# Attention: value products gathered into stretches of two to four token tiles

## The chip, the core and the metric

The kernel runs on one core of a Trainium2 chip. The metric is the device time of one execution in microseconds; a profile comes from one further execution, recorded with its instructions. Names of engines: PE is TensorE (PEld its weight loads), ACT is ScalarE, DVE is VectorE, POOL is GpSimd, SP is SyncE.

## The reference, cut to what matters

Two layers on 1024 tokens of width 1024, each with a mixer and a SwiGLU feed-forward block. The change lies in the first layer's mixer, two kinds of attention side by side, with 8 heads of 64 columns each:

```python
# heads A: softmax over the own chunk of 64 tokens and the 8 before it, learned relative bias
p = jax.nn.softmax(scores, axis=-1)
o = jnp.einsum('bhcqk,bckhd->bhcqd', p, vb)
# heads B: stick-breaking, strictly causal
log_beta = jax.nn.log_sigmoid(z)
log_1m_beta = jnp.where(causal, jax.nn.log_sigmoid(-z), 0.0)
after = lax.cumsum(log_1m_beta, axis=3, reverse=True) - log_1m_beta
w = jnp.where(causal, jnp.exp(log_beta + after), 0.0)
o = jnp.einsum('bhqk,bkhd->bqhd', w, v)
```

The outputs of all heads are joined and go through one output projection. The second layer's mixer is recurrent and, like the feed-forward blocks, isn't touched.

## The kernel before, in words

Heads are handled in pairs, in the order 4, 5, 6, 7, 0, 1, 2, 3 (`seq`): pairs 4 to 7 are the stick-breaking ones (called sigmoid pairs below, after their sigmoid), pairs 0 to 3 the softmax ones. For each pair `project(p)` makes queries and keys (L166 to L168, each product as three fp32r passes of 512 columns), and every second pair `v_tile` makes the values of two pairs (L291 to L293). Then `attend(p)` goes over 8 token tiles of 128 queries:

- scores for the two heads (L364, L365), as wide as the keys that the tile may see: `nb` blocks of 128 keys, 1 to 8 in a sigmoid pair, 1 to 5 in a softmax pair;
- the weights: in a sigmoid pair ScalarE's sigmoid (L372), GpSimd's causal mask (L381), VectorE's reverse scan (L384) and difference (L387); in a softmax pair VectorE's bias and minimum (L368), ScalarE's exponential (L376), VectorE's reciprocal, GpSimd's scaling (L379);
- the `2 * nb` blocks of 128 x 128 weights, two heads in turn, in groups of up to four: four transposes on TensorE into one PSUM tile `tr` of two (L397), a copy to the SBUF tile `pt` of three (L401 on ScalarE, L403 on VectorE for every second group of a softmax tile), and four value products (L406). A value product holds 64 columns of `v` in the array, those of head 0 in one half of it and those of head 1 in the other, and adds 64 rows of `pso`, one PSUM bank for four token tiles;
- after each fourth tile `pso` is copied to `ob` (L412) and stored.

A sigmoid pair has 20 groups, a softmax pair 18.

The order on each engine comes from a planner: the program is traced in the order of its text, and a simulated run of the machine then decides what each engine issues next. Among the instructions whose inputs are there by its clock, the one that stands first in the program goes first; so the projections of the next pair, which stand behind `attend(p)` in the program, are put wherever nothing of the pair itself is ready. TensorE then executes in that order. `issue_after(x)` adds an edge that keeps an instruction behind `x` on the same engine in the issue order; it is no wait for `x` to finish. `behind` does the same for a list. The last pair, 3, has no projections behind it; the output projection's first products (L497) follow.

Of the kernel before, what the change touches and what calls it, by code (L numbers as in the profile page):

```python
# [8 lines left out]
F32 = mybir.dt.float32  # L9
# [6 lines left out]
P = 128  # L16
# [83 lines left out]
class Trunk:  # L100
# [164 lines left out]
    def attention(self, x_src, w_in, bias_t, o_dst, hT):  # L265
        nc, tc = self.nc, self.tc
        with ExitStack() as ctx:
            ap = ctx.enter_context(tc.tile_pool(name="att", bufs=1, reuse_waits="tile"))
# [29 lines left out]
            def v_alloc():  # L298
                return [ap.tile([P, NT, P], F32, tag="v", bufs=3, name=self.uid("v")) for _ in range(2)]
# [27 lines left out]
            def attend(p, st, vt):  # L327
                bias = [None, None]
                if p < 4:
                    for h in range(2):  # L330
                        b = ap.tile([P, 640], F32, tag="bias", bufs=2, name=self.uid("bias"))
                        nc.sync.dma_start(b, bias_t[2 * p + h])
                        nc.gpsimd.tensor_scalar(b, b, -1.0, 1.0, op0=ALU.mult, op1=ALU.mult)
                        nc.gpsimd.memset(b[0:64, 576:640], BIG)
                        nc.gpsimd.memset(b[64:P, 0:64], BIG)
                        bias[h] = b
                for i in range(NT):
                    k0 = max(0, i - 4) if p < 4 else 0
                    nb = i + 1 - k0
                    n = nb * P  # L340
                    if i % 4 == 0:
                        ops = pp.tile([P, 512], F32, tag="o", bufs=1, name=self.uid("pso"))
                    nat = []
                    n_c = 1 if n <= 512 else 2
                    w = n // n_c
                    for h in range(2):
                        qs, k1, k2 = st[h]
                        q = qs[:, i * P:(i + 1) * P]
                        if p < 4 and h == 1:
                            pr = ap.tile([P, 640], F32, tag="nata", bufs=3, name=self.uid("pr"))  # L350
                        else:
                            pr = ap.tile([P, 1024], F32, tag="nat", bufs=4, name=self.uid("pr"))
                        if p < 4:
                            mn = [ap.tile([P, 1], F32, tag="mn", bufs=8, name=self.uid("mn")) for _ in range(n_c)]
                            sm = ap.tile([P, 1], F32, tag="sm", bufs=4, name=self.uid("sm"))
                        for c in range(n_c):
                            if p == seq[-1] and h == 1:

                                sc = prp.tile([P, 512], F32, tag="proj", bufs=2, name=self.uid("sc"))[:, :w]
                            else:  # L360
                                sc = pp.tile([P, 512], F32, tag="sc", bufs=3, name=self.uid("sc"))[:, :w]
                            ks = slice(k0 * P + c * w, k0 * P + c * w + w)
                            cs = slice(c * w, c * w + w)
                            nc.tensor.matmul(sc, q, k1[:, ks], start=True, stop=False)  # L364
                            nc.tensor.matmul(sc, q, k2[:, ks], start=False, stop=True)  # L365
                            if p < 4:
                                off = 640 - n + c * w
                                nc.vector.tensor_tensor_reduce(  # L368
                                    pr[:, cs], sc, bias[h][:, off:off + w], 1.0, 3e38,
                                    op0=ALU.add, op1=ALU.min, accum_out=mn[c])  # L370
                            else:
                                nc.scalar.activation(pr[:, cs], sc, AF.Sigmoid)  # L372
                        if p < 4:
                            if n_c == 2:
                                nc.vector.tensor_tensor(mn[0], mn[0], mn[1], op=ALU.min)
                            nc.scalar.activation(pr[:, :n], pr[:, :n], AF.Exp, bias=mn[0], scale=-1.0,  # L376
                                                 accum_out=sm)
                            nc.vector.reciprocal(sm, sm)
                            nc.gpsimd.tensor_scalar(pr[:, :n], pr[:, :n], sm, 1.0, op0=ALU.mult, op1=ALU.mult)  # L379
                        else:  # L380
                            nc.gpsimd.affine_select(pr[:, n - P:n], pr[:, n - P:n], pattern=[[-1, P]],  # L381
                                                    compare_op=ALU.is_gt, fill=1.0, base=0,
                                                    channel_multiplier=1)
                            nc.vector.tensor_tensor_scan(  # L384
                                pr[:, 0:n][:, ::-1], pr[:, 0:n][:, ::-1], self.zero.to_broadcast([P, n]),
                                1.0, op0=ALU.mult, op1=ALU.add)
                            nc.vector.tensor_tensor(pr[:, 0:n - 1], pr[:, 1:n], pr[:, 0:n - 1],  # L387
                                                    op=ALU.subtract)
                            nc.gpsimd.memset(pr[:, n - 1:n], 0.0)
                        nat.append(pr)  # L390
                    blocks = [(kb, h) for kb in range(nb) for h in range(2)]
                    for b0 in range(0, len(blocks), 4):
                        bl = blocks[b0:b0 + 4]
                        tr = pp.tile([P, 512], F32, tag="tr", bufs=2, name=self.uid("tr"))
                        pt = ap.tile([P, 512], F32, tag="pt", bufs=3, name=self.uid("pt"))
                        for j, (kb, h) in enumerate(bl):
                            nc.tensor.transpose(tr[:, j * P:(j + 1) * P], nat[h][:, kb * P:(kb + 1) * P],  # L397
                                                self.ident)
                        w = len(bl) * P
                        if p >= 4 or (b0 // 4) % 2 == 0:  # L400
                            nc.scalar.copy(pt[:, :w], tr[:, :w])  # L401
                        else:
                            nc.vector.tensor_copy(pt[:, :w], tr[:, :w])  # L403
                        for j, (kb, h) in enumerate(bl):
                            kt = k0 + kb
                            nc.tensor.matmul(  # L406
                                ops[h * 64:(h + 1) * 64, (i % 4) * P:(i % 4) * P + P],
                                vt[p % 2][:, kt, h * 64:h * 64 + 64],
                                pt[:, j * P:(j + 1) * P], start=kb == 0, stop=kb == nb - 1)
                    if i % 4 == 3:  # L410
                        ob = ap.tile([P, 512], F32, tag="ob", bufs=1, name=self.uid("ob"))
                        nc.scalar.copy(ob, ops)  # L412
                        nc.sync.dma_start(o_dst[p][:, (i // 4) * 512:(i // 4) * 512 + 512], ob)

            seq = [4, 5, 6, 7, 0, 1, 2, 3]
            vt = v_alloc()
# [25 lines left out]
            for t, x in enumerate(xt):  # L442
                h = ap.tile([P, D], F32, tag="st", bufs=12, name=self.uid("h0"))
# [18 lines left out]
            for j, p in enumerate(seq):  # L462
                attend(p, st, vt)
                if j < 7:
                    q = seq[j + 1]
                    if q % 2 == 0:
                        wv = v_weights(q // 2)
                        vt = v_alloc()
                        for t2 in range(4):
                            v_tile(q // 2, wv, vt, t2)  # L470
                    st = project(q)
# [675 lines left out]
```

## Time and profile before

| | us |
|---|---|
| median of 3 runs | 2225.85 |
| lowest, highest | 2224.5, 2227.01 |
| the profiled execution | 2226.18 |
| its span, first to last instruction | 2224.4 |
| mean granted TensorE clock | 0.996 |
| first and last value product start | 81.03, 513.9 |

The page gives busy time per engine over the span. A group of the groups' view is one line of the kernel on one engine with one shape: how many, its busy time, the mean length of one in ns, and the idle time of the engine ahead of it with what ended it. TensorE's lengths overlap, since matmuls are pipelined: the distance between two starts says what one holds the engine for. In TensorE's timeline instructions of one line that follow each other without a gap are put together (x8), so a row there is a run.

### The profile page before, as it was taken

What the parts mean: (1) busy time and instruction counts of PE and PEld (TensorE: products, weight loads), DVE (VectorE), ACT (ScalarE), POOL (GpSimd) and SP (SyncE); (2) the same over time, 40 slices, a digit from 0 to 9 for tenths busy, and PEclk for the clock granted to TensorE, in tenths of its full rate; (3) what the DMA queues carried; (4) which work ended last, traced back from release to release, by engine and by line L of the source; (5) the groups of instructions that cost most, each with busy time, mean ns of one, the idle gap of its engine ahead of it and who ended that gap; (6) DMA issues with size and microseconds to landing.
All of it is one profiled execution on the core that took longest, in us unless ns stands there. A gap on an engine that the chain in (4) does not pass through costs nothing. (4 is left out here: it accounts for less than half of the span.)

```text
span 2224.4 us, 30685 instructions
## 1 busy us (share of the span) xinstructions
PE 2191.2 (99%) x11198; PEld 1807.4 (81%) x11198; DVE 1537.5 (69%) x2496; ACT 1146.0 (52%) x2108; POOL 226.8 (10%) x458
## 2 busy tenths in 40 slices
PE   8999999999999999999999999999999999999998
PEld 8887888877788888888888687888788888888886
DVE  5776765464877777775866687636877777768675
ACT  4544455464865444442446568527755444434543
POOL 2111112131100000000001323201100000000011
PEclk9999999999999999999999999999999999999999
DMA  5101011124523333334648611246333333328566
GB/s 167 50 22 42 25 44 41 60 94 139 201 95 95 113 116 96 112 102 170 213 136 256 181 48 48 86 166 206 121 118 114 95 119 95 118 90 284 166 179 161
DMA packets 184393, 266.04 MB, mean 120 GB/s; under 512 B 13617, under 2 KB 114993, under 8 KB 184242
## 3 DMA queue, kind: packets, MB, share of 16 engines
q1 hardware_dynamic: 183602, 261.98, 37.5%
q8 instruction: 88, 1.44, 0.3%
q10 hardware_dynamic: 640, 2.10, 0.3%
q14 instruction: 63, 0.52, 0.1%
HBM read 198.49 MB, written 65.54 MB: 119 GB/s over the span
## 5 line engine op out<-in xcount | busy, mean ns | idle before, releaser
L646 PE MATMUL ps<-hS,q 128*128 128x512 f32 (+1 forms) x1288 | 489.7, 381 | 0.7 <-ACT hS L96 0.3
L647 PE MATMUL ps<-hS,q 128*128 128x512 f32 (+1 forms) x1288 | 489.0, 380 | 0.9 <-DVE hS L89 0.9
L648 PE MATMUL ps<-hS,q 128*128 128x512 f32 (+1 forms) x1288 | 488.4, 380 | 0.0
L617 DVE TENSOR_TENSOR q<-raw,q 128x512 fp32r<-128x512 f32 x308 | 204.5, 685 | 184.7 <-ACT q L616 184.2
L646 PEld LDWEIGHTS ps<-hS,q 128*128 128x128 f32 x1288 | 241.7, 188 | 47.9 <-ACT hS L96 0.7
L647 PEld LDWEIGHTS ps<-hS,q 128*128 128x128 f32 x1288 | 242.2, 188 | 47.3 <-DVE hS L89 1.3
L648 PEld LDWEIGHTS ps<-hS,q 128*128 128x128 f32 x1288 | 242.1, 188 | 45.8
L616 ACT CAST q<-raw 128x512 fp32r<-128x512 f32 x308 | 177.4, 615 | 157.6 <-DVE raw L625 133.2
L732 PE MATMUL ps<-o,o 128*128 128x512 f32 x616 | 239.9, 390 | 0.4 <-DVE o L727 0.2
L733 PE MATMUL ps<-o,o 128*128 128x512 f32 x616 | 238.0, 390 | 0.5 <-DVE o L861 0.5
L604 ACT ACTIVATE raw<-raw,gcol 128x256 f32<-128x256 f32 x352 | 150.3, 498 | 148.9 <-DMA raw<-in_ffn_w_up_dram 73.9
L731 PE MATMUL ps<-o,o 128*128 128x512 f32 x616 | 221.2, 391 | 3.6 <-ACT o L860 3.5
L726 ACT CAST o<-raw 128x512 fp32r<-128x512 f32 x184 | 110.6, 620 | 161.1 <-PE ps L733 51.1
L182 POOL TENSOR_SCALAR rs<-ss 128x1 f32<-128x1 f32 x60 | 32.9, 549 | 1447.1 <-ACT junk L178 1363.0
L727 DVE TENSOR_TENSOR o<-raw,o 128x512 fp32r<-128x512 f32 x184 | 123.1, 686 | 55.6 <-ACT o L726 54.9
L156 DVE TENSOR_TENSOR wlo<-raw,whi 128x1024 fp32r<-128x1024 f32 x76 | 93.0, 1225 | 71.4 <-ACT whi L155 70.1
L731 PEld LDWEIGHTS ps<-o,o 128*128 128x128 f32 x616 | 115.6, 188 | 29.3 <-ACT o L860 5.2
L733 PEld LDWEIGHTS ps<-o,o 128*128 128x128 f32 x616 | 115.7, 188 | 25.3 <-DVE o L861 1.4
L732 PEld LDWEIGHTS ps<-o,o 128*128 128x128 f32 x616 | 115.7, 188 | 25.0 <-DVE o L727 1.2
L155 ACT CAST whi<-raw 128x1024 fp32r<-128x1024 f32 x76 | 79.8, 1051 | 57.2 <-PE ps L167 20.2
L401 ACT COPY pt<-tr 128x512 f32<-128x512 f32 (+1 forms) x128 | 65.5, 528 | 80.3 <-PE tr L397 79.7
L166 PE MATMUL psq<-hT,whi 128*128 128x512 f32 x256 | 101.2, 395 | 1.1 <-DVE v L296 1.1
(202 smaller groups left out, 4336.9 us busy)
## 6 DMA issues: line engine op xcount, KB each, us to landing
raw<-in_ffn_w_gate_dram SPq DMA_DIRECT2D x44, 512.0 KB, 4.2
raw<-in_ffn_w_up_dram SPq DMA_DIRECT2D x44, 512.0 KB, 4.2
gS<-c SPq DMA_DIRECT2D x88, 256.0 KB, 3.9
raw<-gS SPq DMA_DIRECT2D x88, 256.0 KB, 2.8
gA<-c SPq DMA_DIRECT2D x66, 256.0 KB, 3.3
raw<-in_ffn_w_down_dram SPq DMA_DIRECT2D x63, 256.0 KB, 4.0
raw<-in_attn_w_in_dram SPq DMA_DIRECT2D x24, 512.0 KB, 4.1
raw<-gA SPq DMA_DIRECT2D x44, 256.0 KB, 2.9
```

Of the source, the lines that this page charges most:

```text
L166: nc.tensor.matmul(ps, wh[:, kt, cols], hh[:, kt, :], start=kt == 0, stop=False)
L604: nc.scalar.activation(raw[:, i], raw[:, i], AF.Copy, scale=gain[:, 4 * k + i:4 * k + i + 1])
L616: self.last = nc.scalar.copy(t[:, 0], src).ins
L617: self.last_lo = nc.vector.tensor_tensor(t[:, 1], src, t[:, 0].bitcast(F32), op=ALU.subtract).ins
L646: nc.tensor.matmul(ps, a[:, 0, kt, :], bh, start=kt == 0, stop=False)
L647: nc.tensor.matmul(ps, a[:, 0, kt, :], bl, start=False, stop=False)
L648: self.matmul = nc.tensor.matmul(ps, a[:, 1, kt, :], bh, start=False, stop=kt == 3).ins
L726: nc.scalar.copy(t[:, 0], src)
L727: tt(t[:, 1], src, t[:, 0].bitcast(F32), op=ALU.subtract)
L731: nc.tensor.matmul(ps, a[0], b[:, 0], start=first, stop=False)
L732: nc.tensor.matmul(ps, a[0], b[:, 1], start=False, stop=False)
L733: nc.tensor.matmul(ps, a[1], b[:, 0], start=False, stop=last)
```

## The change

In all pairs but the last (`p == seq[-1]`, pair 3), the value products aren't traced behind each group any more but kept in a list, and traced for several token tiles at a stretch: after tiles 3, 5 and 7 in the softmax pairs, after 3, 5, 6 and 7 in the sigmoid pairs. The groups of a stretch come in reverse, the last one first. The first group's products are put behind the last transpose of the tile (`turned`) in TensorE's issue order, and the products of each group behind the last product of the group before. Which product starts and which ends an accumulation is counted by `seen`, as their order is another. `pt` has nine buffers instead of three; the dynamic DMA scratch is set to 2048 bytes, which is less than the default. In the last pair the products follow each group as before.

```diff
+                def values(groups, hold):
+                    for i, nb, k0, bl, pt in groups:
+                        for j, (kb, h) in enumerate(bl):
+                            n = seen[i, h] = seen.get((i, h), 0) + 1
+                            with self.behind(hold):
+                                m = nc.tensor.matmul(
+                                    ops[h * 64:(h + 1) * 64, (i % 4) * P:(i % 4) * P + P],
+                                    vt[p % 2][:, k0 + kb, h * 64:h * 64 + 64],
+                                    pt[:, j * P:(j + 1) * P], start=n == 1, stop=n == nb).ins
+                        if hold:
+                            hold = [m]
+
+                seen, groups = {}, []
+                stretch = () if p == seq[-1] else (3, 5, 7) if p < 4 else (3, 5, 6, 7)
                 for i in range(NT):
...
-                        pt = ap.tile([P, 512], F32, tag="pt", bufs=3, name=self.uid("pt"))
+                        pt = ap.tile([P, 512], F32, tag="pt", bufs=9, name=self.uid("pt"))
                         for j, (kb, h) in enumerate(bl):
-                            nc.tensor.transpose(tr[:, j * P:(j + 1) * P], nat[h][:, kb * P:(kb + 1) * P],
-                                                self.ident)
+                            turned = nc.tensor.transpose(tr[:, j * P:(j + 1) * P],
+                                                         nat[h][:, kb * P:(kb + 1) * P], self.ident).ins
...
-                        for j, (kb, h) in enumerate(bl):
-                            kt = k0 + kb
-                            nc.tensor.matmul(
-                                ops[h * 64:(h + 1) * 64, (i % 4) * P:(i % 4) * P + P],
-                                vt[p % 2][:, kt, h * 64:h * 64 + 64],
-                                pt[:, j * P:(j + 1) * P], start=kb == 0, stop=kb == nb - 1)
+                        groups.append((i, nb, k0, bl, pt))
+                        if not stretch:
+                            values(groups, [])
+                            groups = []
+                    if i in stretch:
+                        values(groups[::-1], [turned])
+                        groups = []
...
-    nc = _bacc.Bacc("TRN2", target_bir_lowering=False, num_devices=1)
+    nc = _bacc.Bacc("TRN2", target_bir_lowering=False, num_devices=1, dynamic_dma_scratch_size=2048)
```

## The prediction

> **What bounds the kernel now.** I read the page first, then the stretches of time in the attention, then the groups there, then TensorE's timeline. The page (engines, and the DMA queues):
>
> ```profile
> span 2224.4 us, 30685 instructions
> PE 2191.2 (99%) x11198; PEld 1807.4 (81%) x11198; DVE 1537.5 (69%) x2496; ACT 1146.0 (52%) x2108; POOL 226.8 (10%) x458
> ...
> q1 hardware_dynamic: 183602, 261.98, 37.5%
> q8 instruction: 88, 1.44, 0.3%
> q10 hardware_dynamic: 640, 2.10, 0.3%
> q14 instruction: 63, 0.52, 0.1%
> ```
>
> TensorE is busy all the way, so what takes time off its instruction stream takes time off the kernel, as long as the others keep up. The busy times by stretch (the attention's own work runs from about 75 to 514 us; four sigmoid pairs to 325, then softmax pairs 0, 1, 2, 3):
>
> ```profile
> core 0: us, PE busy (x) PEld busy (x) DVE busy (x) ACT busy (x) POOL busy (x), PEclk, DMA share, GB/s
> 5.30:8.60 3.30, 2.92 (x13) 1.43 (x11) 1.04 (x2) 1.47 (x3) 0.79 (x2) 1.00 1.01 340
> 75.00:121.00 46.00, 46.00 (x322) 37.98 (x320) 40.49 (x45) 25.83 (x50) 6.47 (x28) 1.00 0.10 30
> 165.00:223.00 58.00, 58.00 (x359) 46.26 (x358) 40.02 (x47) 28.17 (x55) 6.31 (x26) 1.00 0.17 49
> 275.00:325.00 50.00, 50.00 (x347) 41.60 (x343) 32.71 (x40) 26.52 (x49) 4.07 (x16) 1.00 0.17 48
> 420.00:472.00 52.00, 52.00 (x303) 41.76 (x302) 29.05 (x88) 28.27 (x58) 8.63 (x13) 1.00 0.12 41
> 472.00:514.00 42.00, 38.92 (x324) 28.57 (x322) 25.24 (x98) 27.16 (x66) 16.02 (x25) 0.92 0.33 112
> 490.00:492.00 2.00, 2.00 (x10) 1.92 (x9) 1.08 (x5) 1.31 (x6) 0.18 (x1) 0.50 0.31 121
> ```
>
> Up to 472 us TensorE has no idle time: projections of the next pair fill every wait. After that they have run out; in the last 42 us TensorE idles 3.08 and its clock falls to half for a while. VectorE is near its limit in one place, 40.49 of 46 us (88%) in the first pair.
>
> But "busy" counts pipelined instructions, so I measured the distance from one matmul's start to the next. The groups in question, then pieces of TensorE's timeline (start, length, engine, line, shape, how many in a row):
>
> ```profile
> L397 PE MATMUL tr<-ident,pr 128*128 128x128 f32 x528 | 89.0, 286 | 0.0
> L406 PE MATMUL pso<-pt,v 128*64 128x128 f32 x1056 | 85.2, 285 | 1.8 <-ACT pt L401 1.7
> ...
> L401 ACT COPY pt<-tr 128x512 f32<-128x512 f32 x92 | 52.6, 588 | 64.2 <-PE tr L397 63.8
> ...
> L403 DVE COPY pt<-tr 128x512 f32<-128x512 f32 x20 | 13.8, 691 | 20.0 <-PE tr L397 19.9
> L401 ACT COPY pt<-tr 128x256 f32<-128x256 f32 x36 | 13.3, 373 | 16.1 <-PE tr L397 16.0
> ```
>
> ```profile
> 206.93 0.44 PE L406 MATMUL pso<-pt,v 128*64 128x128 f32 x4
> 207.30 0.50 PE L365 MATMUL sc<-st,st 128*128 128x512 f32 x1
> 207.64 0.31 PE L364 MATMUL sc<-st,st 128*128 128x320 f32 x1
> ...
> 209.20 0.39 PE L166 MATMUL psq<-hT,whi 128*128 128x512 f32 x1
> 209.43 0.49 PE L397 MATMUL tr<-ident,pr 128*128 128x128 f32 x3
> 209.67 0.47 PE L167 MATMUL psq<-hT,whi 128*128 128x512 f32 x1
> 209.99 0.39 PE L168 MATMUL psq<-hT,wlo 128*128 128x512 f32 x1
> ...
> 223.38 0.39 PE L166 MATMUL psq<-hT,whi 128*128 128x512 f32 x1
> 223.61 0.40 PE L167 MATMUL psq<-hT,whi 128*128 128x512 f32 x1
> 223.93 0.66 PE L406 MATMUL pso<-pt,v 128*64 128x128 f32 x8
> 224.52 0.98 PE L397 MATMUL tr<-ident,pr 128*128 128x128 f32 x7
> 225.26 0.45 PE L364 MATMUL sc<-st,st 128*128 128x448 f32 x1
> ...
> 230.42 1.09 PE L406 MATMUL pso<-pt,v 128*64 128x128 f32 x16
> 231.45 0.87 PE L397 MATMUL tr<-ident,pr 128*128 128x128 f32 x6
> ```
>
> One value product is two instructions in a row (1056 for 528 blocks), on 64 of the 128 columns (128*64 in the shape). From these rows, the price of one stretch of value products beside its own work:
>
> - Entering: a 512-column matmul is followed after 0.23 us by the next (223.38 to 223.61), but a value product comes 0.32 after it (223.61 to 223.93). +0.09.
> - Inside: 4 instructions take 0.37 to the next start (206.93 to 207.30), 8 take 0.59, 16 take 1.03. So a product costs (1.03 - 0.59)/4 = 0.11, and 0.59 - 4 x 0.11 = 0.15 is fixed.
> - Leaving: the 512-column matmul behind them holds 0.34 (207.30 to 207.64) where 0.23 is normal, +0.11. If transposes follow: three after a projection take 0.24 (209.43 to 209.67) and seven after values 0.74, so (at 0.11 each) the first after values pays +0.06.
>
> A stretch thus costs 0.09 + 0.15 + 0.06 = **0.30 us** with transposes behind it, **0.35** with another matmul. Transposes alone pay nothing: three between projections take 0.24 and the projection behind them 0.32 instead of 0.23, 0.33 for three, their plain 0.11 each.
>
> The Trainium skill (TensorEngine Tiling (Array Packing), Key Properties) says that a change of the array's tiling mode drains it, and its TensorE: Matmul & The Clock Gate, Step-by-step, puts a drain at about 128 cycles; at 2.4 GHz and two changes that would be an estimate of 0.11 us per stretch, and the saving below a third of what it is. The trace shows 0.30, and the trace is used.
>
> How many stretches: I counted runs of L406 in TensorE's timeline, 106 in the first seven pairs and 17 in the last pair, of which these are the first and last of each:
>
> ```profile
> 81.03 0.44 PE L406 MATMUL pso<-pt,v 128*64 128x128 f32 x4
> ...
> 487.75 0.70 PE L406 MATMUL pso<-pt,v 128*64 128x128 f32 x4
> ...
> 493.64 0.44 PE L406 MATMUL pso<-pt,v 128*64 128x128 f32 x4
> ...
> 513.22 1.03 PE L406 MATMUL pso<-pt,v 128*64 128x128 f32 x12
> ```
>
> Of the 106, 95 are followed by transposes and 11 by another matmul: 95 x 0.30 + 11 x 0.35 = 32.4 us, mere switching.
>
> **The change part by part.** *Stretches.* Values are held back until the last transpose of token tiles 3, 5, 7 (softmax) or 3, 5, 6, 7 (sigmoid), each group behind the one before: 3 x 3 + 4 x 4 = 25 stretches. The last group goes first, so the copy that lands last is awaited once and the rest is ready. One exception: in softmax pairs the middle group is copied by VectorE (691 ns) and started only shortly before ScalarE's short last one (373 ns); a projection may slip in there. I take 3 splits over nine stretches, 28 in all (bounds 25 and 34). All are followed by scores or projections: 28 x 0.35 = 9.8. Saved: 32.4 - 9.8 = 22.6 us. It lies thus: sigmoid pairs 57 x 0.30 + 8 x 0.35 - 16 x 0.35 = 14.3; softmax to 472 us 29 x 0.30 + 2 x 0.35 - 10 x 0.35 = 5.9; pair 2 behind 472 us 9 x 0.30 + 0.35 - 2 x 0.35 = 2.4. The last pair keeps its order (its list of stretches is empty).
>
> *The end without projections.* There TensorE waits for copies and reductions:
>
> ```profile
> 481.66 0.44 PE L406 MATMUL pso<-pt,v 128*64 128x128 f32 x4 [1.34 <-ACT pt L401]
> ...
> 486.82 0.69 PE L364 MATMUL sc<-st,st 128*128 128x384 f32 x1 [1.29 <-DVE mn L368]
> ```
>
> so I count the 2.4 us there as nothing: VectorE's and ScalarE's chains set the pace. The bounds: the half clock lasts 486.6 to 493.4 us, work of 3.4 us taking 6.8; with the values of tiles 6 and 7 now filling the idle time it may go (-3.4), or come once more (+3.4).
>
> *Waits that faster TensorE meets.* In the sigmoid pairs every window is full (46.00 of 46.00); with 14.3 us less in 250 VectorE goes from 88% to about 93% in the first. Where the scan is late, transposes at the head of TensorE's queue hold the projections behind them. Bounds: 0, and half of the 14.3, since VectorE's free 5.5 us in the first window shrink to about half. I take 2.0, half a microsecond per sigmoid pair, nearer the rows that show no wait at all.
>
> *The hold itself.* The first product of a stretch waits for its copy; behind it in TensorE's order stand the next tile's scores, and behind these ScalarE's sigmoids and VectorE's reductions. Projections are ready to be put in that gap, at no cost; without them it would be the 1.34 us above. It is out of reach of the last pair.
>
> *Nine buffers.* A stretch holds at most 6 groups (tiles 0 to 3: 1+1+2+2; tiles 4 and 5: 3+3), so 3 are left for the next tile's copies, as many as there were. Copies, their engines and their number stay. *The store* of four tiles' output comes out with the stretch; nothing waits for it before the output projection, and the accumulator bank is needed again only at the stretch of tile 5 instead of at once. No DMA is added or moved past another on SP's queue. *The scratch*: every queue in the rows above is a hardware or an instruction queue, so nothing uses it; 0, both ends.
>
> Sum: 22.6 - 2.4 - 2.0 = **18.2 us**. The profiled execution took 2226.18 us (span 2224.4, 1.8 around it), 0.3 above the median of the runs. 2226.2 - 18.2 = **2208.0**. Its own range: without waits and without the half clock 2226.2 - 22.6 - 3.4 = 2200; with half of the sigmoid part lost 2213.
>
> **The rivals.**
>
> 1. *VectorE sets the pace.* The saving turns into waits of TensorE in the sigmoid pairs, 7.2 us, and the clock falls once more at the end: 20.2 - 7.2 - 3.4 = 9.6, 2216.5 us. For it: 88% in the first pair. Against: 65 to 69% in the windows from 165 and 275, and full windows now.
> 2. *The stretches fall apart.* The planner that orders TensorE's instructions puts projections between the groups, as the copies come. With 32.4/0.35 = 92 stretches nothing is gained: 2226. For it: many groups stand alone now. Against: they stand alone because a group and the transposes two groups on wait for the same copy; behind the hold the copies are done.
> 3. *Each stretch begins with a wait* (slower). The hold puts the values right behind the transposes whose copy they need, and if the planner sees that copy done earlier than it is, TensorE stands still for 1.34 us (481.66) 25 times: 33.5 - 22.6 = +10.9, 2237 us. It decides from 22.6/25 = 0.9 us a stretch on. For it: two such waits at the end. Against: none before 472 us in 96 stretches.
> 4. *The clock falls where transposes run without values between them*, at the end, twice more: +6.8, 2215 us. The Trainium skill (TensorE: Matmul & The Clock Gate, PE-mode transpose) says that transposes don't count as activity for the clock. Against that rule stands the start, where almost nothing but transposes ran and the clock was at 1.00 from 5.3 us (the first window above):
>
> ```profile
> 1.34 2.40 PE L433 MATMUL warm<-ident 128*128 128x128 f32 x10 [1.34 <-POOL ident masks.py:199]
> 3.53 2.77 PE L440 MATMUL warm<-ident 128*128 128x128 f32 x16
> ```
>
> **How the numbers follow.** Forecast 0.64, rival 1 0.17, rival 4 0.05, rival 2 0.08, rival 3 0.06. Forecast and rivals 1 and 4 are faster by more than 0.2% (4.5 us, about what a measurement of this kernel can tell from no change): 0.86; rival 2 the same: 0.08; rival 3 slower: 0.06. The range runs from 2201 to 2219: it takes in rivals 1 and 4 and leaves out 2 and 3 and the edges.
>
> **What would show it.** Right: about 25 to 34 runs of L406 in the first seven pairs, most of 28 to 44 instructions, the group's 1056 instructions unchanged; 0.23 us from projection to projection around lone transposes; the first product of the last pair some 18 us earlier than 493.64; everything behind the attention of the same length. Rival 1: idle time before L397 and L364 put down to VectorE. Rival 2: 60 or more runs. Rival 3: idle time before L406 put down to the copies of L401. Rival 4: a granted clock below 0.92 behind the last projection. The prediction is wrong if the runs are as few as I say and the attention is not 10 us shorter, or if the gain is more than 23 us and so has another source.

## The result, and the profile after

The changed kernel takes 2207.63 us (median of 5 runs, 2206.03 to 2207.69) against 2225.85 before: ratio 0.9919, 95% interval 0.9909 to 0.993. The forecast was 2208.0. Its profiled execution has a span of 2205.9 us, 18.5 less. The same rows of the page as before:

```profile
span 2205.9 us, 30596 instructions
PE 2171.6 (98%) x11198; PEld 1811.9 (82%) x11198; DVE 1535.9 (70%) x2496; ACT 1144.1 (52%) x2108; POOL 228.6 (10%) x458
```

TensorE has the same 11198 matmuls and is busy 19.6 us less. To see where, I cut both profiles at three instructions that the program fixes: the attention's first score, its last projection (L168) and its last value product. Busy time by stretch between them, before:

```profile
68.92:472.00 403.08, 403.08 (x2895) 336.62 (x2894) 264.98 (x479) 206.59 (x418) 68.78 (x185) 1.00 0.13 39
472.00:513.97 41.97, 38.89 (x323) 28.54 (x322) 25.24 (x98) 27.16 (x66) 16.02 (x25) 0.92 0.33 112
```

and after (columns as in the prediction: start and end, length, then PE, PEld, DVE, ACT and POOL busy, granted clock, DMA share, GB/s):

```profile
69.67:452.32 382.65, 381.59 (x2872) 337.74 (x2871) 263.44 (x477) 204.65 (x417) 71.20 (x185) 1.00 0.13 42
452.32:494.39 42.07, 38.53 (x345) 30.02 (x344) 25.32 (x101) 27.39 (x65) 15.08 (x25) 0.92 0.30 107
```

Ahead of the first score 0.75 us were lost (68.92 to 69.67). From the first score to the last projection, called the main stage from here on, 403.08 - 382.65 = **20.43 us** were won. The end without projections is as long as it was, 42.07 against 41.97. From the last value product to the end of the span it is 2205.9 - 494.4 = 1711.5 against 2224.4 - 514.0 = 1710.4; two further profiles of the order before gave 1712.4 and 1718.0 there, so that 1.1 us says nothing. Nor do the 0.75 us ahead of the first score: further profiles have it at 69.9 and 69.3 with the order before, and at 69.0 twice with the order after. The main stage, on the other hand, repeats to 0.1 us in every further profile of one order; it is the measure that the experiments are read by, beside the whole time.

The stretches themselves, on TensorE's timeline after (L344 are the value products now, L413 the transposes, L380 and L381 the scores):

```profile
98.08 0.33 PE L381 MATMUL sc<-st,st 128*128 128x384 f32 x1
98.34 2.40 PE L344 MATMUL pso<-pt,v 128*64 128x128 f32 x40
100.68 0.55 PE L413 MATMUL tr<-ident,pr 128*128 128x128 f32 x3
...
115.73 2.62 PE L344 MATMUL pso<-pt,v 128*64 128x128 f32 x44
118.28 0.55 PE L413 MATMUL tr<-ident,pr 128*128 128x128 f32 x3
```

40 instructions take 2.34 us from start to start, 20 products at 0.11 and 0.14 over, so the fixed price inside is still paid once. Counted over the whole timeline, the first seven pairs have 25 runs of L344, none split, 22 of them with transposes behind them and 3 with another matmul; in the main stage lie 23 (20 and 3), where 96 lay before (86 and 10). The last pair has 15 (17 before).

What is new are waits. First the groups of values and transposes after, then the places, on TensorE's timeline:

```profile
L413 PE MATMUL tr<-ident,pr 128*128 128x128 f32 x528 | 84.5, 278 | 3.3 <-ACT pt L417 1.9 <-DVE pr L403 1.0 <-POOL pr L395 0.4
L344 PE MATMUL pso<-pt,v 128*64 128x128 f32 x1056 | 68.8, 282 | 0.2 <-ACT pt L417 0.2
```

```profile
127.82 0.99 PE L413 MATMUL tr<-ident,pr 128*128 128x128 f32 x6
128.84 0.45 PE L380 MATMUL sc<-st,st 128*128 128x384 f32 x1
...
133.70 0.30 PE L413 MATMUL tr<-ident,pr 128*128 128x128 f32 x1 [0.48 <-DVE pr L403]
...
253.11 0.30 PE L413 MATMUL tr<-ident,pr 128*128 128x128 f32 x1 [0.48 <-DVE pr L403]
```

VectorE's difference (L403) is late twice, for the third token tile of the second and of the fourth sigmoid pair, some microseconds behind the last stretch of the pair before; in the main stage of before TensorE had no idle time at all. Not all of a wait shows as idle time: the six transposes at 127.82 hold TensorE 1.02 us where about 0.57 would do (five times 0.11, and 0.03 for the last, whose time lies in the score behind it), and no idle time is noted. Value products wait for their copies 0.2 us in all, once, at 486.51 in the last pair; inside the stretches of the main stage no wait is noted.

### The profile page after: what moved, and what is told of

It is laid out like the page before. It is cut to its first block, busy times and chain, and to the rows that moved or that the text cites. A ratio compares the mean times of both kernels' runs of the same rounds, so it can differ in the third digit from the quotient of the medians.

```text
span 2205.9 us, 30596 instructions
## 1 busy us (share of the span) xinstructions
PE 2171.6 (98%) x11198; PEld 1811.9 (82%) x11198; DVE 1535.9 (70%) x2496; ACT 1144.1 (52%) x2108; POOL 228.6 (10%) x458
## 5 line engine op out<-in xcount | busy, mean ns | idle before, releaser
L400 DVE TENSOR_TENSOR_SCAN pr<-pr,zero 128x128 f32<-128x128 f32 (+7 forms) x64 | 87.0, 1364 | 28.1 <-POOL pr L397 27.8
```

## The experiments

Two theories of the gain stood against each other: **switches** (each stretch of value products costs 0.30 us with transposes behind it, whatever else happens) and **order or buffers** (transposes run ahead, fewer waits). All times were taken beside the kernel before on the same chip, so the ratios are compared; 0.1% is 2.2 us.

**Cutting the stretches.** The most direct test puts the same 109 idle transposes of the identity, into a tile that nothing reads, either between the groups or behind them:

```diff
+ cut = pp.tile([P, 512], F32, tag="tr", bufs=2, ...)
  for g, (i, nb, k0, bl, pt) in enumerate(groups):
      ...                                    # the group's products
+     if hold and g < len(groups) - 1:       # cut: between the groups
+         with self.behind(hold):
+             m = nc.tensor.transpose(cut[:, 0:P], self.ident, self.ident).ins
+         hold = [m]
# twin: the same len(groups) - 1 transposes in a loop behind the last group
```

> The changed kernel with one transpose of the identity put between any two groups of a stretch in the first seven pairs, 109 in all; each cuts the stretch, so there are 134 instead of 25. Its twin has the same 109 transposes behind the stretches. Theory of switches: 109 x 0.30 = 33 us more than the twin, and 45 us more than the changed kernel with 0.11 us for each transpose, about 2252. Rival (the stretches' length isn't what matters): both the same, about 2219.6.

> The twin: the 109 transposes of the identity behind the last group of each stretch, three to five in a row, 25 stretches as in the changed kernel. Both theories: 109 x 0.11 = 12 us more than the changed kernel, about 2219.6.

Cut: 2253.84 us, ratio 1.013 (1.0113 to 1.0147). Twin: 2221.24, ratio 0.9986 (0.9977 to 0.9995). The difference on one chip is 32.6 us; 33 was expected. The cut of one stretch of 20 products, on TensorE's timeline (L345 the products, L353 the cuts):

```profile
97.33 0.33 PE L386 MATMUL sc<-st,st 128*128 128x384 f32 x1
97.59 0.66 PE L345 MATMUL pso<-pt,v 128*64 128x128 f32 x8
98.18 0.33 PE L353 MATMUL cut<-ident 128*128 128x128 f32 x1
98.44 0.66 PE L345 MATMUL pso<-pt,v 128*64 128x128 f32 x8
...
101.61 0.44 PE L345 MATMUL pso<-pt,v 128*64 128x128 f32 x4
101.98 0.66 PE L418 MATMUL tr<-ident,pr 128*128 128x128 f32 x4
```

and the same stretch in the twin:

```profile
98.14 2.40 PE L345 MATMUL pso<-pt,v 128*64 128x128 f32 x40
100.47 0.77 PE L354 MATMUL cut<-ident 128*128 128x128 f32 x5
101.08 0.60 PE L419 MATMUL tr<-ident,pr 128*128 128x128 f32 x4
```

The 20 products and five idle transposes take 101.98 - 97.59 = 4.39 us cut and 101.08 - 98.14 = 2.94 whole: 1.45 for five cuts, 0.29 each, with equal instructions and no idle time. That the price belongs to changing between value products and other matmuls, and not to anything that the products wait for, is shown by this pair. The twin is 0.67% above the changed kernel, 15 us; the transposes' own 12 and waits make it up.

That the whole came to 32.6 is in part luck. Main stage and end, first of the cut kernel, then of the twin:

```profile
68.80:492.76 423.96, 421.56 (x2964) 348.27 (x2962) 263.34 (x472) 204.17 (x413) 71.67 (x184) 1.00 0.12 37
492.76:541.29 48.53, 44.33 (x363) 32.31 (x362) 27.07 (x105) 29.23 (x70) 16.00 (x26) 0.89 0.28 95
```

```profile
69.34:465.75 396.41, 393.32 (x2974) 348.82 (x2973) 265.96 (x480) 206.46 (x418) 72.73 (x185) 1.00 0.13 40
465.75:508.41 42.66, 38.09 (x354) 30.12 (x352) 25.82 (x98) 27.72 (x65) 15.10 (x25) 0.96 0.31 110
```

The main stages are 27.6 us apart for 99 of the cuts, which at 0.30 would be 29.7; six transposes and four scores, about 1.3 us of work, lie behind the cut kernel's main stage instead of in it, and TensorE is idle 2.40 us there against 3.09. The ends are 5.9 apart for the other 10 cuts, with that work and a lower clock (0.89 against 0.96) in it.

The pair leaves one question: a value product differs from its neighbours in its 64 columns, but it is also a product of plain fp32 in two instructions, and its neighbours are transposes and fp32r products. The kernel before answers it further on, in the output projection, where fp32 products of two instructions each, on 128 columns (L497), stand between transposes (L222):

```profile
593.30 1.04 PE L222 MATMUL pst<-ident,mg 128*128 128x128 f32 x8
594.18 1.88 PE L497 MATMUL ps<-raw,act 128*128 128x512 f32 x4
595.89 1.04 PE L222 MATMUL pst<-ident,mg 128*128 128x128 f32 x8
596.77 1.88 PE L497 MATMUL ps<-raw,act 128*128 128x512 f32 x4
```

Eight transposes take 0.88 from start to start both times, 0.11 each, and four product instructions 1.71, 0.43 each: nothing is paid on entering or leaving. So it is the change between 64 and 128 columns of stationary data that costs, and not the change to fp32 products. Whether it matters that the 64 columns lie in one half of the array, now in this one and now in the other, no run separates.

**Buffers without the order.**

```diff
-  pt = ap.tile([P, 512], F32, tag="pt", bufs=3, ...)      # the kernel before
+  pt = ap.tile([P, 512], F32, tag="pt", bufs=9, ...)
-  nc = _bacc.Bacc("TRN2", ..., num_devices=1)
+  nc = _bacc.Bacc("TRN2", ..., num_devices=1, dynamic_dma_scratch_size=2048)
```

> The kernel before with nine buffers of transposed weights and the 2 KB scratch, value products as they were. Theory of switches: the gain is the number of stretches alone, so this has the 123 stretches of before and its time, 2225.9 us within 0.2%. Rival (buffers): the transposes get ahead because copies no longer wait for a buffer; then this alone takes a good part of the 18 us, 2210 to 2220.

Ratio 1.0002 (0.9993 to 1.0011). The planner gives every engine the order of before, and the windows of this run read

```profile
69.90:473.00 403.10, 403.10 (x2894) 336.61 (x2893) 265.05 (x479) 207.20 (x417) 69.03 (x185) 1.00 0.13 39
473.00:511.50 38.50, 36.48 (x324) 26.25 (x322) 24.68 (x98) 27.08 (x66) 16.09 (x25) 1.00 0.36 122
```

The main stage is that of before, 403.10 against 403.08. Nine buffers and the small scratch are worth nothing by themselves; the rival falls.

**Fewer buffers with the order**: `bufs=6` in the changed kernel.

> The changed kernel with six buffers, as many as a stretch holds; TensorE's planned order is the same. What I wrote: three buffers beside the six held are what keeps the copies going. If that is so, each stretch holds the next tile's copies up: with 25 stretches and a wait of 0.2 to 0.4 us each, 2212 to 2218. Rival: the copies of the next tile come after the stretch anyway, 2207.6 within 2.

Ratio 0.9915 (0.99 to 0.993), main stage:

```profile
69.00:451.70 382.70, 381.65 (x2873) 337.73 (x2872) 263.40 (x477) 204.75 (x417) 70.33 (x185) 1.00 0.13 41
```

Same as with nine. My sentence that three buffers beside the six keep the next tile's copies going is wrong: nothing waits for them.

**The hold.** Without the edges (`values(groups[::-1], [])`) the program that comes out is the same, instruction for instruction, on every engine, so this was not run. It is the place in the program and the reversed order that make the stretches; the edges are satisfied anyway.

**One stretch per tile** (`stretch = tuple(range(NT))` in the first seven pairs).

> The changed kernel with a stretch after each token tile in the first seven pairs: 56 stretches there instead of 25. Theory of switches: 31 more at 0.30 us, 9.3 us more than the changed kernel, about 2216.9. Rival (order): what helped is that values stand behind the transposes at all; then one stretch per tile does as well, about 2208.

2223.78 us, ratio 0.9972 (0.996 to 0.9983): 0.53% above the changed kernel, 11.8 us where 9.3 were expected. The main stage:

```profile
69.10:462.00 392.90, 389.27 (x2869) 335.49 (x2868) 263.15 (x470) 204.68 (x414) 64.78 (x184) 1.00 0.13 40
```

It is 10.2 us longer. In it lie 52 stretches (43 with transposes behind, 9 without): 43 x 0.30 + 9 x 0.35 = 16.1 against 20 x 0.30 + 3 x 0.35 = 7.1, so 9.0 are switches. Four scores of 320 columns less lie in the stage, at 0.15 each, so waits are 10.2 - 9.0 + 0.6 = 1.8 longer; TensorE is idle 3.63 us here and 1.06 in the changed kernel. Values behind their transposes alone aren't the gain.

**Forward order** (`values(groups, [turned])`).

> The changed kernel with the groups of a stretch in forward order, first group first. In TensorE's planned order the first seven pairs have 49 stretches then instead of 25. Theory of switches: 24 more at 0.30 us, 7.2 us more than the changed kernel, about 2214.8. Rival (waits): the reversed order gains because no stretch stands still inside; then the cost shows as idle time before value products, put down to the copies, and isn't 0.30 per stretch.

2216.6 us, ratio 0.9935 (0.9921 to 0.9948): 3.6 us above the changed kernel, half of what was expected. The main stage:

```profile
69.10:455.90 386.80, 386.79 (x2870) 337.24 (x2869) 261.91 (x467) 205.74 (x413) 72.09 (x184) 1.00 0.13 41
```

Its 46 stretches (28 and 18) cost 28 x 0.30 + 18 x 0.35 = 14.7, 7.6 more than the changed kernel's, and it is 4.1 longer. Of the missing 3.5, 0.6 are work (four scores less lie in the stage here too). The other 2.9 are waits that this order hasn't: TensorE is idle for 0.01 us in it. So the long stretches cost about 3 us of waits, and the reversed order is a good bargain, not a free one. The rival falls on its own sign: there is no idle time before value products here.

**The last pair too** (`() if p == seq[-1] else` taken out).

> The changed kernel with stretches after tiles 3, 5 and 7 in the last pair too: 3 stretches there instead of 15. Theory (the end without projections is paced by VectorE's and ScalarE's chains): the 12 switches saved, 3.6 us, give nothing, 2207.6 within 2. Rival (TensorE paces the end as well): 2204. Second rival: values held back leave TensorE nothing to do in the waits, 2210 or more.

Ratio 0.9921 (0.9907 to 0.9934), the changed kernel's time. The end without projections has 12 stretches less and is not shorter:

```profile
450.50:493.70 43.20, 36.67 (x344) 30.35 (x344) 25.65 (x101) 27.34 (x65) 15.08 (x25) 0.92 0.29 104
```

TensorE is idle 6.53 us in it instead of 3.54: what it no longer spends on switches it spends waiting. Whether TensorE doesn't pace this end, or the values held back cost as much in new waits as the switches gave (the second rival, at a lower price), this run doesn't tell apart. That TensorE's speed counts for nothing there isn't shown either: the one profile that has the full clock throughout this end, the one with nine buffers above, is 3.5 us shorter in it.

**Fewer and longer stretches.** Two versions with more buffers; the second takes the output tile from them:

```diff
-  stretch = ... (3, 5, 7) if p < 4 else (3, 5, 6, 7)
+  stretch = ... (3, 5, 7)                     # eleven
+  stretch = ... (3, 7) if p < 4 else (3, 5, 7)   # twelve
-  pt = ap.tile([P, 512], F32, tag="pt", bufs=9, ...)
+  pt = ap.tile([P, 512], F32, tag="pt", bufs=11, ...)   # twelve: 12, and ob from the same tag
-  dynamic_dma_scratch_size=2048
+  dynamic_dma_scratch_size=1024
```

> The changed kernel with eleven buffers (scratch 1 KB) and the sigmoid pairs' tiles 6 and 7 in one stretch: 21 stretches in the first seven pairs instead of 25. Theory of switches: 4 x 0.30 = 1.2 us less, about 2206.4. Rival: eight groups held of eleven buffers make copies wait for buffers and transposes for copies, 2208 or more.

> Eleven buffers and 21 stretches again. Its first run was 3.0 us shorter than the changed kernel from the first score to the last projection (379.7), where four switches explain 1.2; the rest would be shorter waits in the sigmoid pairs, which belong to the order and so come again: 379.7 in that stage, and 2 to 4 us less than the changed kernel in all. Rival: the rest was chance, and the whole is 1.2 us less.

> Twelve buffers (the output tile ob is one of them) and in the softmax pairs 0 and 1 the tiles 4 to 7 in one stretch, as well as the sigmoid pairs' tiles 6 and 7: in the first seven pairs 19 stretches in TensorE's order instead of 21. Theory of switches: 2 x 0.30 = 0.6 us less than with eleven, in that stage 379.1. Rival (as 12 groups are held and no buffer is left, copies and transposes wait): 381 or more in that stage.

> The changed kernel unchanged, beside the two below on one chip, so that they can be compared with it directly. From the first score to the last projection 382.7 us, as in its first profile; 0.9919 of the kernel before.

The last three ran side by side: changed kernel 2207.59 us, ratio 0.9921 (0.9908 to 0.9935), eleven 2205.93, 0.9912 (0.9898 to 0.9925), twelve 2203.43, 0.9901 (0.9887 to 0.9914); eleven had 0.9899 (0.9884 to 0.9913) the first time. The main stages, changed kernel again, eleven again, twelve:

```profile
69.00:451.70 382.70, 381.63 (x2873) 337.78 (x2872) 263.80 (x477) 204.63 (x417) 69.82 (x185) 1.00 0.13 41
```

```profile
69.40:449.10 379.70, 379.32 (x2868) 337.26 (x2867) 262.92 (x471) 204.55 (x415) 74.51 (x185) 1.00 0.14 42
```

```profile
68.70:447.60 378.90, 378.32 (x2870) 337.64 (x2869) 262.27 (x476) 203.65 (x416) 72.34 (x185) 1.00 0.13 42
```

Eleven is 3.0 us shorter in the stage, both times: 4 x 0.30 = 1.2 are switches, 0.6 are four scores of 320 columns less in the stage, and the other 1.2 are shorter waits (0.38 us idle instead of 1.07). The timeline shows which: the two waits of 0.48 us for VectorE's difference are gone, and a few microseconds ahead of those two places a shorter one for a copy has come, of which this is the first:

```profile
126.60 0.41 PE L413 MATMUL tr<-ident,pr 128*128 128x128 f32 x2 [0.17 <-ACT pt L417]
```

Why, the runs don't tell. On the whole time eleven came out 1.7 us below the changed kernel where 2 to 4 were expected, and the two intervals overlap widely: its gain is shown for the stage alone. Twelve has the shortest stage of all, 378.9 where 379.1 was expected, 3.8 below the changed kernel. On the whole time its median is 4.2 us lower, but the intervals overlap a little, so there its gain is likely and not shown.

**The kernel before once more**, for the end.

> The kernel before, one more profile. With nine buffers it had the same order on every engine, the same 403.1 us from the first score to the last projection, but 38.5 us instead of 42.0 from there to the last value product, without the half clock there. If the half clock at the end is a matter of where a fixed grid of time falls, this profile has 403.1 again and either 38.5 or 42.0; if the buffers are what shortened the end, it has 42.0 with the half clock.

```profile
69.30:472.30 403.00, 403.00 (x2894) 336.58 (x2893) 265.01 (x479) 206.63 (x417) 68.78 (x185) 1.00 0.13 39
472.30:513.20 40.90, 39.24 (x322) 27.97 (x322) 24.70 (x98) 27.29 (x66) 16.01 (x25) 0.92 0.33 115
```

Neither answer: 40.9, with the half clock (0.92 over the window) and 1.66 us idle. With nine buffers the same order had 38.5 at a clock of 1.00. One profile each can't separate the buffers from where the clock's change falls; this stays open.

## Why the prediction was right, point by point

*The price of a stretch*, 0.30 us, was read from starts and measured again by the cuts, 0.29 to 0.30. The estimate of 0.11 in the prediction would have made 12 us of the 32.6 between the cut kernel and its twin. It is also a little over a third of 0.30, and not below a third, as the prediction has it. The Trainium skill (TensorEngine Tiling (Array Packing), Key Properties) states a drain at each change of tiling mode. The runs agree that the change between 64 and 128 columns costs time, 0.29 to 0.30 us a stretch; that the time is a drain, no run here shows.

*The number of stretches* was 25 where I took 28, and what follows them is mostly transposes where I wrote that all would be followed by scores or projections: 22 x 0.30 + 3 x 0.35 = 7.7 us of switching left instead of 9.8. This term was mis-sized by 2.1 us, to the cautious side. The first product of the last pair starts at 473.83 instead of 493.64, 19.8 earlier where some 18 was forecast. The reason behind the sentence failed too: when the values are issued, the first transposes of the next tile are ready, and they come before projections in the program.

*The waits* were mis-sized the other way. In the main stage, switches fell from 86 x 0.30 + 10 x 0.35 = 29.3 us to 7.1, by 22.2. Four transposes, eight products and two scores of 320 columns less lie in it, as projections end earlier in the program's course: 12 x 0.11 + 2 x 0.15 = 1.6 more, a term that the sum didn't have. It became 20.4 shorter, so waits took 22.2 + 1.6 - 20.4 = 3.4, where I had put 2.0. The rows at 127.82, 133.70 and 253.11 show some of it in the place that rival 1 named, the sigmoid pairs, released by VectorE's difference; the forward order, without idle time, shows most of the sum (2.9) from the other side. Rival 1 was thus there, at less than half of its price (7.2).

*The end* was put at nothing, and so it came: 42.07 against 41.97, at the same clock of 0.92; in the run with stretches in the last pair the switches saved turned into idle time. What sets its length isn't settled: the order before took 42.0, 40.9 and, once, at the full clock, 38.5. So the prediction's reason, that VectorE's and ScalarE's chains set the pace there, is not shown.

*The hold and the nine buffers* were costed at nothing, rightly, but for reasons that fell: the edges change no order, and six buffers do.

*The other rivals.* The stretches didn't fall apart (25 runs, rival 2). Stretches don't wait for their copies (rival 3): the 0.2 us before L344 stand in the last pair; the reversed order makes the last copy the only one in question. The clock in the end is 0.92 as before (rival 4), though transposes run there without values between them.

Terms against measurement: 20.2 of switches and -2.0 of waits in the main stage, 18.2 forecast there; 22.2 + 1.6 - 3.4 = 20.4 measured. Then, in this one profile, 0.75 us were lost ahead of the attention and 1.1 behind it, which the forecast had at nothing and which are no more than scatter. That the whole came within half a microsecond is in part luck: three terms missed by 1 to 2 us each, two of them up and one down, and the scatter took off most of what was left.

## What to carry to other kernels

Read an engine that is busy 99% by the distances between starts: the same matmul costs more behind one of another shape, and the surplus times the number of changes is what regrouping can win, up to the point where the regrouped work makes others wait. Cut a stage at instructions that the program fixes; such a stage repeated to 0.1 us here, where the whole time of one kernel spread over 7 us. Count what lies in such a stage, too: two orders of one program had a few scores more or less in it, and 0.6 us of work looked like a wait. And check a saving for where it lies: the same switches saved where TensorE had waits already gave nothing.

## What the runs showed of the hardware

A stretch of fp32 products on 64 columns among matmuls on 128, at the full granted clock, costs 0.09 us on entering, 0.15 inside, and 0.06 (transposes next) or 0.11 (a 512-column product next) on leaving; nearly all of it shows in no idle time and no wait, only in starts. Fp32 products on 128 columns between fp32 transposes pay no such price. A lone fp32 transpose between fp32r products costs its plain 0.11. Waits too can hide: of some 3.4 us in the main stage the profile gives 1.06 as idle.
